# Attention's output kept as 512 rows with its sums apart, and a state tensor with its slots innermost

## The chip, the cores and the metric

The kernel runs on one core of a Trainium2 chip. The metric is the time of one execution on the device, in microseconds (us). The core has five engines with an instruction queue each: TensorE (PE; its weight loads are listed as PEld), VectorE (DVE), ScalarE (ACT), GpSimd (POOL) and SyncE (SP). SP computes nothing here; it issues nearly all DMA transfers, one after the other, and an instruction that waits holds up everything behind it in its queue. The same holds for the queues of the other engines.

## The reference

Two layers of a backbone over 1024 latent tokens with 256 context tokens in front, 1280 columns in all (T in the kernel). Only layer 0 is touched by the change. There attention and a state-space layer (S5) work side by side on parts of one projection, and their outputs are put together and projected:

```python
def _softmax_attend(q, k, v):
    s = einsum('bqhd,bkhd->bhqk', q, k) * MLA_SCALE
    return einsum('bhqk,bkhd->bqhd', softmax(s), v)          # 8 heads of 64 values

def _s5_states(u, lb_re, lb_im, bb_re, bb_im, h0):           # 32 groups, 64 complex states, two directions
    x_re, x_im = einsum(u, bb_re), einsum(u, bb_im)
    s_re, s_im = associative_scan(_s5_combine, (a, x))       # s[t] = lb * s[t-1] + x[t], complex

def s5_out(y, us):
    z = gelu(y + d_g * us)
    return z * sigmoid(z @ w_glu)

y_lat = concat([att_l, s5_out(ys_l, us_l)], -1) @ w_out      # and the same for the context tokens
```

Then come LayerNorm, a gated convolutional FFN, the second layer (HGRN2) and its FFN.

## The kernel before

All of it is one program; its instructions are put in order ahead of time, engine by engine, by a list scheduler that works with a model of durations. So the order on an engine is fixed when the kernel runs, and an edit can move instructions far from it. Large products are made of three fp32r matmuls on a high and a low part (`mm3`, L103 to L105; `split` at L111 and L114 makes the parts).

**Attention** (`attention`, L694). For each head `qk(h + 1)` (keys, queries, and the row maxima `mx`, L796) is interleaved with `attend(h)` (L811 on): for a block of up to 512 queries and every tile of 128 keys, three matmuls into `pS`, an Exp on ACT (L821), the split into `ph` and `pl` on ACT and on DVE or POOL in turn (L114), and three matmuls into `po` (L826 to L828). Row 64 of `po` is the sum of the exponentials. The block `ao`, 65 rows, goes to the DRAM tensor `attd[h]` (L834), which is 8 x 65 x 1280. `inverse` (L842) reads the sums of two heads from `attd` into `rsum`, 128 partitions of up to 20 numbers (L847), takes the reciprocal on DVE (L849) and writes it to the DRAM tensor `rsd` (L850). It is called after heads 1, 3 and 5, and for the last pair after each of the three blocks of head 7.

**S5** (`S5Half.run`, L883) is interleaved with the heads. It works on half of the groups at a time (`hh` = 0, 1), with 1280 columns in 160 chunks of 8. Per half:

- 8 steps of matmuls `pV` (L904) give the chunk inputs; ACT writes them to `H` (L907).
- A scan over the 160 chunks: two levels up (`both((0, 1), True)`), 38 sequential steps on POOL (L946, L948, L949), two levels down. In the levels direction 0 runs on DVE and direction 1 on POOL, each a product into `t` (L923) and two additions into `H` (L927). Tile `t` carries the tag of `RO` on DVE and of `Tm` on POOL, and is so named in the profile.
- 16 groups of matmuls `pY`: 4 that read `H` (L965) and one that reads `U` (L968). An fp32 matmul is two passes, so these are 8 and 2 PE instructions a group, 256 and 64 in all. Then a gelu on ACT and DVE (L969 to L974) and a write to the DRAM tensor `Zd` (L977). All groups share one PSUM bank.

`H` is 128 x 161 x 2 x 2 x 8: slot (chunk) outermost, then direction, real or imaginary part, and 8 group pairs innermost. One slot is 32 numbers, 128 bytes. So the scan's operands are runs of 16 or 8 neighbours, and a `pY` matmul reads 160 numbers that are 128 bytes apart.

**mix_out0** (L1191) follows. It loads `z` from `Zd` (L1200), and for each block of columns the attention values (`acc<-attd`, L1215, into a part of `acc` that is free then) and the reciprocals (`r<-rsd`, L1216). `zs` is the split of `z` on ACT (L1219) and DVE (L1220). The reciprocals are spread over partitions by a matmul with `sel` (`prs`, L1224) and multiplied on (L1226). `pglu` (L1232 on) is the gate product. `mix_out` (`pmix`) then makes the output projection. For the second and third block the loads at L1215 stand behind `k.last_inv` in the order (`behind`, L127).

Of the kernel before, what the change touches and what calls it, by code (L numbers as in the profile page):

```python
# [693 lines left out]
def attention(k, A):  # L694
# [115 lines left out]
    def attend(h):  # L810
        b = h % 2  # L811
        q, kk_, v = QT[b], KT[b], Vt[b]
        for s, e in BLK:
# [19 lines left out]
            nc.scalar.activation(o[0:65, :n], po[0:65, :n], AF.Copy)  # L833
            nc.sync.dma_start(out=k.attd[h, :, s:e], in_=o[0:65, :n])  # L834
            yield 1
            if h == 7:
                inverse(h, s, e)
        if h in (1, 3, 5):
            inverse(h, 0, T)
            yield 1  # L840

    def inverse(h, s, e):  # L842

        n = (e - s) // 64
        r = AO([128, 20], tag="rsum")
        a, o = k.attd, k.rsd
        nc.sync.dma_start(out=r[:, :n], in_=bass.AP(tensor=a.tensor, offset=a.offset + ((h - 1) * 65 + 64) * T + s,  # L847
                                                    ap=[[65 * T, 2], [n, 64], [1, n]]))
        nc.vector.reciprocal(r[:, :n], r[:, :n])  # L849
        k.last_inv = nc.sync.dma_start(out=bass.AP(tensor=o.tensor, offset=o.offset + (h - 1) * T + s,  # L850
                                                   ap=[[T, 2], [n, 64], [1, n]]), in_=r[:, :n])

# [18 lines left out]
class S5Half:  # L871
# [11 lines left out]
    def run(self):  # L883
        k, nc, P = self.k, self.k.nc, self.P
        E = nc.gpsimd
        for hh in range(2):
            U = P([128, 16, 160], tag="U")
            for j in range(8):
                nc.sync.dma_start(out=U[16 * j:16 * j + 16],
                                  in_=k.Sd[hh * 16:hh * 16 + 16, :, j].rearrange("g c x -> c g x"))  # L890
            H = P([128, 161, 2, 2, 8], tag="H")
            Mh = P([128, 3, 2, 2, 2, 8], tag="Mh")
# [4 lines left out]
            for p in range(8):  # L897
                RT = P([128, 2, 2, 128], tag="RO", bufs=2)
                nc.sync.dma_start(out=RT[:], in_=k.s5R[hh * 8 + p].rearrange("d i s x -> s d i x"))
                for d in range(2):  # L900
                    ps = bank(k, "pV", "D")
                    for i in range(2):
                        for q in range(2):
                            nc.tensor.matmul(ps[64 * q:64 * q + 64, i * 160:i * 160 + 160],  # L904
                                             lhsT=RT[:, d, i, 64 * q:64 * q + 64], rhs=U[:, 2 * p + q], start=True, stop=True)
                    o = 1 - d
                    nc.scalar.activation(H[:, o:o + 160, d, :, p].rearrange("p x i -> p i x"),  # L907
                                         ps[:, :320].rearrange("p (i x) -> p i x", i=2), AF.Copy)
# [4 lines left out]
            def bulk(i, up, d):  # L913
# [5 lines left out]
                for j in range(0, 80 // h, m):  # L919
                    n = min(m, 80 // h - j)  # L920
                    t = P([128, m, 2, 16], tag=tag, bufs=2 - d)[:, :n]
                    at = lambda s0, dims: raw(H, (s0 + 2 * h * j) * 32 + 16 * d, [[64 * h, n]] + dims)
                    e.tensor_tensor(t, Mh[:, i, d].rearrange("p a b q -> p a (b q)").unsqueeze(1)  # L923
                                    .to_broadcast([128, n, 2, 16]), at(src, [[0, 2], [1, 16]]), op=OP.mult)
                    o = at(dst, [[8, 2], [1, 8]])
                    for b in range(2):
# [8 lines left out]

            nc.vector.memset(H[:, 160, 1], 0.0)
            yield from both((0, 1), True)
            nc.vector.memset(H[:, 128, 0], 0.0)
            seq = [(128 + c, 132 + c, (132 + c) % 160) for c in range(4, 32, 4)] + [(c, c + 4, c + 4) for c in range(0, 124, 4)]
            seb = [(c + 4, c) for c in range(152, 0, -4)]  # L940
            assert len(seq) == len(seb)
            for (pf, cf, df), (pb, cb) in zip(seq, seb):
                sl = lambda f, b, dims: raw(H, f * 32, [[(b - f) * 32 + 16, 2]] + dims)
                t1 = P([128, 2, 2, 2, 8], tag="t1", bufs=2)
                t2 = P([128, 2, 16], tag="t2", bufs=2)
                E.tensor_tensor(t1[:].rearrange("p d a b q -> p d a (b q)"), Mh[:, 2].rearrange("p d a b q -> p d a (b q)"),  # L946
                                sl(pf, pb, [[0, 2], [1, 16]]), op=OP.mult)
                E.tensor_tensor(t2[:].rearrange("p d (a q) -> p d a q", a=2), t1[:, :, :, 0], t1[:, :, :, 1], op=OP.add)  # L948
                E.tensor_tensor(sl(df, cb, [[1, 16]]), t2[:], sl(cf, cb, [[1, 16]]), op=OP.add)  # L949
                yield 1  # L950
            yield from both((1, 0), False)
            for p in range(8):
# [8 lines left out]
                for q in range(2):  # L961
                    ps = bank(k, "pY", "D")
                    for d in range(2):
                        for i in range(2):
                            nc.tensor.matmul(ps[:, :160], lhsT=O[64 * q:64 * q + 64, d, i],  # L965
                                             rhs=H[64 * q:64 * q + 64, d:d + 160, d, i, p],
                                             start=d == 0 and i == 0, stop=False)
# [223 lines left out]
def mix_out0(k, A, u, acc):  # L1191
# [11 lines left out]
    for s, e in BLK:  # L1203
# [8 lines left out]
        for ct in range(4):  # L1212
            for i in range(n // w):
                with behind(k, k.last_inv if s else None):
                    nc.sync.dma_start(out=at[ct][:, i], in_=k.attd[2 * ct:2 * ct + 2, 0:64, s + i * w:s + i * w + w])  # L1215
        nc.sync.dma_start(out=rt[:, :n], in_=k.rsd[:, s:e])  # L1216
        zs = [G([128, 4, 512], R, tag=f"zs{i}", bufs=1) for i in range(2)]
# [332 lines left out]
def body(tc, A, out, stop=None, taps=None):  # L1550
# [11 lines left out]
    with ExitStack() as st:  # L1562
# [4 lines left out]
        k.Zd = tc.dram_tile([32, 16, 8, 160], F, name="Zd")  # L1567
        k.attd = tc.dram_tile([8, 65, T], F, name="attd")
        k.rsd = tc.dram_tile([8, T], F, name="rsd")
        wp = k.wip  # L1570
# [111 lines left out]
```

## Time and profile before

| what | value |
|---|---|
| time, median of 3 runs (lowest to highest) | 3838.55 us (3833.25 to 3847.12) |
| the profiled execution's own time | 3833.38 us |
| its span, first to last instruction | 3831.3 us |
| mean granted TensorE clock | 0.962 |
| busy: PE, DVE, ACT, POOL | 3622.7, 2061.9, 1090.9, 1135.5 us |

The times are of single executions. The span leaves out 2 us around the first and last instruction. The busy share of an engine is an average over stages with different limits; matmuls are pipelined, so a busy PE is not one at its best rate. The stage that the change touches, attention with S5 beside it and then mix_out0, lies between about 250 and 1030 us of the span.

### The profile page before, as it was taken

To read this page: it belongs to the slowest core of one execution; us is meant where nothing else is said; L and a number is where in the kernel's file an instruction comes from. 1 tells how busy PE (TensorE), PEld (TensorE's weight loads), DVE (VectorE), ACT (ScalarE), POOL (GpSimd) and SP (SyncE) were. 2 spreads that over 40 slices of the span, in tenths; PEclk is the share of its full clock that TensorE was granted. 3 is DMA by queue.
4 is the path that set the end of the run, shared out by engine and by line. 5 is a ranking of instruction groups with operands and counts; after the bars stand their busy time and mean duration, and the time that the engine had idled before them with its cause. 6 is when DMAs were issued, how large, how long until landed. Compare 5 with 4: busy or idle time off the path is not lost.

```text
span 3831.3 us, 47488 instructions
## 1 busy us (share of the span) xinstructions
PE 3622.7 (95%) x19081; PEld 2926.6 (76%) x19081; DVE 2061.9 (54%) x3297; ACT 1090.9 (28%) x1798; POOL 1135.5 (30%) x1089
## 2 busy tenths in 40 slices
PE   6987999997799999999999999999999999999997
PEld 4764566565588888888887888999987978888885
DVE  7836745773445444444446756464654654444445
ACT  2323435443323111121112422222222421212113
POOL 3617612851243111211113511111112622222222
PEclk9997989998899999999999999999998999999998
DMA  7462335312311111111110211111113111111111
GB/s 241 121 172 79 110 93 138 108 37 69 122 39 34 34 39 34 40 43 39 39 34 28 78 34 34 34 34 34 34 49 96 44 55 39 55 44 50 44 44 44
DMA packets 295583, 243.13 MB, mean 63 GB/s; under 512 B 42496, under 2 KB 256858, under 8 KB 294338
## 3 DMA queue, kind: packets, MB, share of 16 engines
q1 hardware_dynamic: 290434, 227.40, 20.0%
q10 hardware_dynamic: 4928, 12.69, 1.0%
q8 instruction: 150, 2.46, 0.3%
q14 instruction: 71, 0.58, 0.0%
HBM read 203.83 MB, written 38.32 MB: 63 GB/s over the span
## 4 chain that ended last, share of the span: by engine, by line
PE 83%; DVE 5%; DMA 3%; POOL 2%; issue 1%; ACT 1%; SPq 0%; ACTq 0%; POOLq 0%; DVEq 0%
PE pa L105 5%; PE pa L103 5%; PE pa L104 5%; PE po L103 5%; PE pg L103 5%; PE pg L105 5%; PE pg L104 5%; PE po L104 5%; PE po L105 5%; PE ph L104 3%; PE ph L105 3%; PE ph L103 3%; PE pA L1433 3%; PE pY L965 2%; PE pmix L103 1%; PE pmix L105 1%
## 5 line engine op out<-in xcount | busy, mean ns | idle before, releaser
L114 POOL TENSOR_TENSOR w<-ws,w 128x1024 fp32r<-128x1024 f32 (+1 forms) x205 | 500.9, 2449 | 1567.6 <-ACT w L111 1389.3
L1066 DVE SCALAR_TENSOR_TENSOR acc<-po,mod,acc 128x512 f32<-128x512 f32 (+1 forms) x456 | 309.3, 679 | 557.9 <-PE po L105 557.6
L103 PE MATMUL po<-hh,w 128*128 128x512 f32 (+1 forms) x912 | 342.1, 376 | 9.8 <-DVE acc L1066 8.1
L104 PE MATMUL po<-hl,w 128*128 128x512 f32 (+1 forms) x912 | 335.6, 368 | 6.0 <-DVE hl L114 6.0
L105 PE MATMUL po<-hh,w 128*128 128x512 f32 (+1 forms) x912 | 335.0, 368 | 0.0
L111 ACT ACTIVATE w<-ws 128x1024 fp32r<-128x1024 f32 (+1 forms) x207 | 216.9, 1049 | 409.9 <-PE pg L105 164.6
L103 PE MATMUL pa<-uh,w 128*128 128x512 f32 (+1 forms) x896 | 331.7, 370 | 0.9 <-ACT w L111 0.8
L104 PE MATMUL pa<-ul,w 128*128 128x512 f32 (+1 forms) x896 | 330.1, 369 | 0.1
L105 PE MATMUL pa<-uh,w 128*128 128x512 f32 (+1 forms) x896 | 326.4, 370 | 0.8 <-POOL w L114 0.8
L103 PE MATMUL pg<-uh,w 128*128 128x512 f32 (+1 forms) x872 | 324.1, 372 | 2.0 <-ACT w L111 2.0
L104 PE MATMUL pg<-ul,w 128*128 128x512 f32 (+1 forms) x872 | 322.6, 370 | 0.0
L105 PE MATMUL pg<-uh,w 128*128 128x512 f32 (+1 forms) x872 | 321.5, 372 | 0.6 <-POOL w L114 0.6
L103 PE MATMUL ph<-uh,w 128*128 128x512 f32 (+1 forms) x624 | 238.9, 383 | 1.1 <-ACT uh L1052 1.1
L104 PE MATMUL ph<-ul,w 128*128 128x512 f32 (+1 forms) x624 | 236.1, 378 | 1.3 <-DVE ul L1054 1.3
L105 PE MATMUL ph<-uh,w 128*128 128x512 f32 (+1 forms) x624 | 235.2, 377 | 0.0
L103 PEld LDWEIGHTS po<-hh,w 128*128 128x128 f32 x912 | 173.2, 190 | 45.3 <-DVE acc L1066 11.1
L104 PEld LDWEIGHTS po<-hl,w 128*128 128x128 f32 x912 | 173.9, 191 | 38.1 <-DVE hl L114 7.0
L105 PEld LDWEIGHTS po<-hh,w 128*128 128x128 f32 x912 | 173.7, 190 | 30.2
L103 PEld LDWEIGHTS pa<-uh,w 128*128 128x128 f32 x896 | 168.7, 188 | 32.7 <-ACT w L111 1.0
L105 PEld LDWEIGHTS pa<-uh,w 128*128 128x128 f32 x896 | 168.6, 188 | 32.2 <-POOL w L114 1.3
L104 PEld LDWEIGHTS pa<-ul,w 128*128 128x128 f32 x896 | 168.6, 188 | 32.2 <-DVE ul L1054 0.3
L103 PEld LDWEIGHTS pg<-uh,w 128*128 128x128 f32 x872 | 164.1, 188 | 35.6 <-ACT w L111 2.4
(401 smaller groups left out, 7914.6 us busy)
## 6 DMA issues: line engine op xcount, KB each, us to landing
ws<-in_ffn_w_in_dram SPq DMA_DIRECT2D x88, 512.0 KB
adaw<-in_ada_w_dram SPq DMA_DIRECT2D x80, 512.0 KB
ws<-in_ffn_w_out_dram SPq DMA_DIRECT2D x44, 512.0 KB
ws<-in_hg_w_in_dram SPq DMA_DIRECT2D x40, 512.0 KB
w<-in_ada_w_dram SPq DMA_DIRECT2D x8, 1024.0 KB
ws<-in_ev_w_out_dram SPq DMA_DIRECT2D x10, 512.0 KB
ws<-in_hg_w_out_dram SPq DMA_DIRECT2D x10, 512.0 KB
ws<-in_ev_w_in_dram SPq DMA_DIRECT2D x9, 512.0 KB
```

What stands on the lines that cost most here:

```text
L103: nc.tensor.matmul(ps, lhsT=w[0], rhs=x[0], start=start, stop=False)
L104: nc.tensor.matmul(ps, lhsT=w[0], rhs=x[1], start=False, stop=False)
L105: return nc.tensor.matmul(ps, lhsT=w[1], rhs=x[0], start=False, stop=stop)
L111: nc.scalar.activation(hi, src, AF.Copy)
L114: (nc.gpsimd if elo == "p" else nc.vector).tensor_tensor(lo, src, hi.bitcast(F), op=OP.subtract)
L965: nc.tensor.matmul(ps[:, :160], lhsT=O[64 * q:64 * q + 64, d, i], rhs=H[64 * q:64 * q + 64, d:d + 160, d, i, p], start=d == 0 and i == 0, ...
L1066: k.nc.vector.scalar_tensor_tensor(a, ps[:, :e - s], modcol(k, layer, seg, 1 if s >= SEQ else 0, ct), a, op0=OP.mult, op1=OP.add)
L1433: nc.tensor.matmul(ps[:, i * 128:i * 128 + 128], lhsT=km[:, c:c + 128], rhs=raw(Q, c, [[2 * hs, 64 // hs], [SEQ + hs, 2], [1, hs]]), start ...
```

## The change

Two independent edits.

1. `attd` becomes 512 x 1280 (head and value as rows), and the sums go to a tensor of their own, `atts`, 8 x 1280: each block is written by two DMAs, of 64 rows and of 1 row. `inverse` is gone. `mix_out0` loads 128 rows of `attd` at a time, loads the sums as 8 rows, and takes the reciprocal there, on the tile of 8 partitions x up to 512. The loads of the later blocks stand behind `k.last_sum`, the last write of sums.
2. `H` becomes 128 x 2 x 2 x 8 x 161: direction, part, pair, and the slot innermost. Neighbours in the slot are adjacent; neighbours in the pair are 161 numbers (644 bytes) apart. Every operand of `H` is rewritten for that; counts and sizes of instructions stay.

```diff
-            nc.sync.dma_start(out=k.attd[h, :, s:e], in_=o[0:65, :n])
+            nc.sync.dma_start(out=k.attd[64 * h:64 * h + 64, s:e], in_=o[0:64, :n])
+            k.last_sum = nc.sync.dma_start(out=k.atts[h:h + 1, s:e], in_=o[64:65, :n])
             yield 1
-            if h == 7:
-                inverse(h, s, e)
-        if h in (1, 3, 5):
-            inverse(h, 0, T)
-            yield 1
...
-            H = P([128, 161, 2, 2, 8], tag="H")
+            H = P([128, 2, 2, 8, 161], tag="H")
...
-                    nc.scalar.activation(H[:, o:o + 160, d, :, p].rearrange("p x i -> p i x"),
+                    nc.scalar.activation(H[:, d, :, p, o:o + 160],
...
-                    at = lambda s0, dims: raw(H, (s0 + 2 * h * j) * 32 + 16 * d, [[64 * h, n]] + dims)
+                    at = lambda s0, dims: raw(H, s0 + 2 * h * j + 16 * 161 * d, [[2 * h, n]] + dims)
-                                    .to_broadcast([128, n, 2, 16]), at(src, [[0, 2], [1, 16]]), op=OP.mult)
-                    o = at(dst, [[8, 2], [1, 8]])
+                                    .to_broadcast([128, n, 2, 16]), at(src, [[0, 2], [161, 16]]), op=OP.mult)
+                    o = at(dst, [[8 * 161, 2], [161, 8]])
...
-                E.tensor_tensor(sl(df, cb, [[1, 16]]), t2[:], sl(cf, cb, [[1, 16]]), op=OP.add)
+                E.tensor_tensor(sl(df, cb, [[161, 16]]), t2[:], sl(cf, cb, [[161, 16]]), op=OP.add)
...
-                                             rhs=H[64 * q:64 * q + 64, d:d + 160, d, i, p],
+                                             rhs=H[64 * q:64 * q + 64, d, i, p, d:d + 160],
...
-                with behind(k, k.last_inv if s else None):
-                    nc.sync.dma_start(out=at[ct][:, i], in_=k.attd[2 * ct:2 * ct + 2, 0:64, s + i * w:s + i * w + w])
-        nc.sync.dma_start(out=rt[:, :n], in_=k.rsd[:, s:e])
+                with behind(k, k.last_sum if s else None):
+                    nc.sync.dma_start(out=at[ct][:, i], in_=k.attd[128 * ct:128 * ct + 128, s + i * w:s + i * w + w])
+        nc.sync.dma_start(out=rt[:, :n], in_=k.atts[:, s:e])
+        nc.vector.reciprocal(rt[:, :n], rt[:, :n])
...
-        k.attd = tc.dram_tile([8, 65, T], F, name="attd")
-        k.rsd = tc.dram_tile([8, T], F, name="rsd")
+        k.attd = tc.dram_tile([512, T], F, name="attd")
+        k.atts = tc.dram_tile([8, T], F, name="atts")
```

The scheduler gives the attention stage a new order. Outside it, nearly nothing moves. Three places matter.

SP's queue at the end of attention, before: the writes of the last two blocks of head 7, the loads of attention values, and the reads and writes of `inverse` stand ahead of the load of `z`.

```order
L834 DMA attd<-ao 65x512
L1215 DMA acc<-attd 128x1x512
L847 DMA rsum<-attd 128x1x8
L834 DMA attd<-ao 65x256
L1215 DMA acc<-attd 128x1x512
L850 DMA rsd<-rsum 2x64x8
L1215 DMA acc<-attd 128x1x512 x2
L847 DMA rsum<-attd 128x1x4
L850 DMA rsd<-rsum 2x64x4
L1215 DMA acc<-attd 128x1x256 x2
L1200 DMA z<-Zd 128x1280 x4
```

The same place now (L962 is the write to `Zd`, L1200 the load of attention values, L1185 the load of `z`):

```order
L834 DMA attd<-ao 64x256
L943 DMA RO<-s5O 128x4x128
L835 DMA atts<-ao 1x256
L1200 DMA acc<-attd 128x512
L1200 DMA acc<-attd 128x256 x2
L962 DMA Zd<-z 8x16x160 x2
L1200 DMA acc<-attd 128x256 x6
L962 DMA Zd<-z 8x16x160 x4
L1185 DMA z<-Zd 128x1280 x4
```

The chain through `rsum` and `rsd` is gone; the last three pairs of writes to `Zd`, which stood ahead of the last block of attention, now stand behind it.

PE at the end of attention, before: the last group of `pY` (L965, L968), the last tiles of head 7, and the first `pglu`.

```order
L965 MATMUL pY<-H,RO 128x160 x4
L968 MATMUL pY<-U,Tm 128x160
...
L826 MATMUL po<-ph,V_2164 128x256
L827 MATMUL po<-ph,V_2165 64x256
L828 MATMUL po<-pl,V_2164 128x256
L103 MATMUL pglu<-zs_8214,w 128x512 x2
```

And now (L950 and L953 are the two kinds of `pY`); the pair of `pY` rows comes six times behind the last tile of attention:

```order
L826 MATMUL po<-ph,V_2164 128x256
L827 MATMUL po<-ph,V_2165 64x256
L828 MATMUL po<-pl,V_2164 128x256
L950 MATMUL pY<-H,RO 128x160 x4
L953 MATMUL pY<-U,Tm 128x160
...
L103 MATMUL pglu<-zs_8215,w 128x512 x2
```

Six of the 16 groups of the second half have moved behind attention. Counted in tiles of `attend` (176 in all), the first `pY` of the two halves stands behind tile 36 and 154 now, where it stood behind 32 and 142.

DVE at the start of mix_out0, before: two reciprocals of `inverse`, then the splits of `z`.

```order
L849 RECIPROCAL rsum<-rsum 128x8
L849 RECIPROCAL rsum<-rsum 128x4
L1220 TENSOR_TENSOR zs_8215<-z,zs_8214 128x512 x4
L1226 TENSOR_TENSOR rt<-acc,prs 128x512 x2
L1237 TENSOR_TENSOR sg<-sg,z 128x512
```

And now (L1206 is the split, L1202 the reciprocal, L1212 the product with `prs`, L1223 the gate):

```order
L1206 TENSOR_TENSOR zs_8216<-z,zs_8215 128x512 x3
L1202 RECIPROCAL r_8208<-r_8208 8x512
L1206 TENSOR_TENSOR zs_8216<-z,zs_8215 128x512
L1212 TENSOR_TENSOR rt<-acc,prs 128x512 x2
L1223 TENSOR_TENSOR sg<-sg,z 128x512
L1212 TENSOR_TENSOR rt<-acc,prs 128x512
L1223 TENSOR_TENSOR sg<-sg,z 128x512
L114 TENSOR_TENSOR ul<-sg,uh 128x512
L1212 TENSOR_TENSOR rt<-acc,prs 128x512
L1202 RECIPROCAL r_8322<-r_8322 8x512
```

The reciprocals stand between the splits and the products of the blocks, each behind a load of 8 rows.

## Rows read from the trace of the kernel before

**Rows 1.** Busy us (count) of each engine, clock, DMA: stretches of PE's matmuls.
```profile
452.00:578.00 126.00, 126.00 (x541) 77.94 (x540) 59.99 (x104) 49.20 (x106) 21.62 (x24) 0.91 0.33 95
716.00:785.00 69.00, 68.36 (x386) 43.48 (x386) 45.09 (x80) 37.68 (x71) 58.66 (x132) 1.00 0.34 104
835.00:927.00 92.00, 92.00 (x353) 64.60 (x352) 40.07 (x65) 43.13 (x96) 17.23 (x13) 0.89 0.24 68
933.00:972.00 39.00, 0.00 (x0) 0.00 (x0) 0.38 (x2) 1.04 (x2) 0.00 (x0) 0.51 0.33 107
```

**Rows 2.** The same for the first of the scan's four level stretches, and their sum.
```profile
306.00:340.00 34.00, 18.31 (x61) 10.16 (x61) 31.96 (x47) 5.81 (x10) 26.64 (x27) 0.59 0.10 27
...
sum 171.00, PE 135.09 PEld 84.11 DVE 156.04 ACT 66.10 POOL 136.77; mean PE 33.77 PEld 21.03 DVE 39.01 ACT 16.52 POOL 34.19
```

**Rows 3.** Chain that ended last, end of attention: start us, us, what.
```profile
932.22 2.29 DMA attd<-ao
934.53 6.63 DMA rsum<-attd
...
941.42 6.05 DMA rsd<-rsum
947.49 10.42 DMA rsum<-attd
...
959.88 11.45 DMA z<-Zd
```

**Rows 4.** ACT in order of time, the last of the four splits of z.
```profile
976.76 1.12 ACT L1219 ACTIVATE zs<-z 128x512 fp32r<-128x512 f32 x1 [0.53 <-DMA z<-Zd]
```

**Rows 5.** PE in order of time: start us, us; one group of pY.
```profile
463.77 2.42 PE L965 MATMUL pY<-H,RO 64*128 64x160 f32 x8
466.12 0.54 PE L968 MATMUL pY<-U,Tm 128*128 128x160 f32 x2
```

**Rows 6.** The same: fp32 passes over 128 neighbouring numbers, in layer 1.
```profile
2264.68 1.95 PE L1455 MATMUL pO<-AT,V 128*128 128x128 f32 x16
2266.46 0.49 PE L1472 MATMUL pT<-ident,K 128*128 128x128 f32 x3
```

**Rows 7.** Groups by form, the scan: xcount | busy us, mean ns | idle before.
```profile
L927 DVE TENSOR_TENSOR H<-H,RO 128x256 f32<-128x256 f32 x56 | 46.4, 840 | 0.3
L923 DVE TENSOR_TENSOR RO<-Mh,H 128x512 f32<-128x512 f32 x28 | 25.9, 929 | 4.0 <-POOL H L949 3.6 <-ACT H L907 0.4
...
L927 POOL TENSOR_TENSOR H<-H,Tm 128x320 f32<-128x320 f32 x48 | 50.9, 1060 | 2.4
L923 POOL TENSOR_TENSOR Tm<-Mh,H 128x640 f32<-128x640 f32 x24 | 42.7, 1778 | 3.0 <-ACT H L907 1.7
L946 POOL TENSOR_TENSOR t<-Mh,H 128x64 f32<-128x64 f32 x76 | 28.5, 376 | 5.2
L949 POOL TENSOR_TENSOR H<-t,H 128x32 f32<-128x32 f32 x76 | 24.6, 323 | 5.0
```

**Rows 8.** Groups by form, DVE at L1443: steps of 8 and of 16 bytes.
```profile
L1443 DVE TENSOR_TENSOR F<-F 128x1280 f32<-128x1280 f32 x8 | 11.9, 1489 | 0.2
L1443 DVE TENSOR_TENSOR F<-F 128x640 f32<-128x640 f32 x8 | 10.8, 1352 | 0.2
```

**Rows 9.** Groups by form, ACT from PSUM: steps of 128 bytes, and none.
```profile
L907 ACT ACTIVATE H<-pV 128x320 f32<-128x320 f32 x32 | 23.7, 740 | 27.4 <-PE pV L904 26.8 <-ACT vo L728 0.4
L1474 ACT ACTIVATE kt<-pT 128x384 f32<-128x384 f32 x48 | 23.3, 488 | 58.7 <-PE pT L1472 58.6
```

**Rows 10.** Busy us (count), clock, DMA share, GB/s; mix_out0's first block.
```profile
985.00:990.00 5.00, 5.00 (x21) 3.69 (x20) 5.00 (x6) 3.27 (x6) 2.68 (x2) 1.00 0.13 44
```

**Rows 11.** SP in order of time: six loads of attention values.
```profile
969.91 21.30 SPq L1215 DMA_DIRECT2D acc<-attd  x6
```

**Rows 12.** PE in order of time: the second block's reciprocals.
```profile
1000.98 2.90 PE L1224 MATMUL prs<-r,sel 8*128 8x512 f32 x3 [8.21 <-DMA r<-rsd]
```

**Rows 13.** Groups by form, DVE's reciprocals.
```profile
L849 DVE RECIPROCAL rsum<-rsum 128x8 f32<-128x8 f32 x2 | 0.4, 203 | 10.4 <-DMA rsum<-attd 10.4
L434 DVE RECIPROCAL sm<-sm 128x32 f32<-128x32 f32 x1 | 0.3, 347 | 0.0
```

More of the change, by code (lines that the diff above doesn't have):

```diff
@@ L833, in attend @@
             nc.scalar.activation(o[0:65, :n], po[0:65, :n], AF.Copy)
-            nc.sync.dma_start(out=k.attd[h, :, s:e], in_=o[0:65, :n])
+            nc.sync.dma_start(out=k.attd[64 * h:64 * h + 64, s:e], in_=o[0:64, :n])
+            k.last_sum = nc.sync.dma_start(out=k.atts[h:h + 1, s:e], in_=o[64:65, :n])
             yield 1
-            if h == 7:
-                inverse(h, s, e)
-        if h in (1, 3, 5):
-            inverse(h, 0, T)
-            yield 1
[L842 to L851, printed above, removed]
     AD = Pool(k, "ada1", "right")
@@ L934, in both @@
                     yield 1
-            nc.vector.memset(H[:, 160, 1], 0.0)
+            nc.vector.memset(H[:, 1, :, :, 160], 0.0)
             yield from both((0, 1), True)
-            nc.vector.memset(H[:, 128, 0], 0.0)
+            nc.vector.memset(H[:, 0, :, :, 128], 0.0)
             seq = [(128 + c, 132 + c, (132 + c) % 160) for c in range(4, 32, 4)] + [(c, c + 4, c + 4) for c in range(0, 124, 4)]
@@ L942, in run @@
             for (pf, cf, df), (pb, cb) in zip(seq, seb):
-                sl = lambda f, b, dims: raw(H, f * 32, [[(b - f) * 32 + 16, 2]] + dims)
+                sl = lambda f, b, dims: raw(H, f, [[b - f + 16 * 161, 2]] + dims)
                 t1 = P([128, 2, 2, 2, 8], tag="t1", bufs=2)
@@ L946, in run @@
                 E.tensor_tensor(t1[:].rearrange("p d a b q -> p d a (b q)"), Mh[:, 2].rearrange("p d a b q -> p d a (b q)"),
-                                sl(pf, pb, [[0, 2], [1, 16]]), op=OP.mult)
+                                sl(pf, pb, [[0, 2], [161, 16]]), op=OP.mult)
                 E.tensor_tensor(t2[:].rearrange("p d (a q) -> p d a q", a=2), t1[:, :, :, 0], t1[:, :, :, 1], op=OP.add)
-                E.tensor_tensor(sl(df, cb, [[1, 16]]), t2[:], sl(cf, cb, [[1, 16]]), op=OP.add)
+                E.tensor_tensor(sl(df, cb, [[161, 16]]), t2[:], sl(cf, cb, [[161, 16]]), op=OP.add)
                 yield 1
```

## The prediction

> **What bounds the kernel now.** I read the busy times by stretch first. In 452 to 578 us and 835 to 927 us, where the `pY` groups stand between attention's tiles, PE is busy all the time, DVE less than half, POOL under a fifth [rows 1]: PE sets the pace. In the sequential scan (716 to 785 us) it is busy 68.36 of 69 us, with POOL at 58.66. In the four stretches of the scan's levels it is not: of 171 us DVE is busy 156.04, POOL 136.77, PE 135.09, and in the first of them PE only 18.31 of 34 [rows 2]; there attention's own DVE work queues behind the scan's. From 933 to 972 us PE does nothing [rows 1]. The chain of waits tells why [rows 3]: the last block of sums is read back (6.63 us), written (6.05 us), the next read lands 10.42 us after its issue, and only then does SP reach the load of `z`, which takes 11.45 us more. The last split of `z` starts at 976.76 us [rows 4].
>
> **Part 1: `pY` reads neighbours.** A pass of L965 takes (466.12 - 463.77) / 8 = 0.294 us for 160 numbers 128 bytes apart [rows 5]. An fp32 pass over 128 neighbours takes (2266.46 - 2264.68) / 16 = 0.111 us [rows 6], so 0.139 us for 160. The difference is 0.155 us, over 256 passes 39.7 us. Both ends: nothing, if the width of 64 rows and not the step makes these passes slow; 39.7 us otherwise. I take the latter, since 0.294 is twice what the count asks for. Of the 32 groups 26 still lie ahead of attention's end: 26 x 8 x 0.155 = 32.2 us. The six that moved behind it leave that stretch wholly: 6 x (2.35 + 0.54) = 17.3 us. Together 49.5 us of PE's queue. PE bounds most of the stretch but not the levels, where its share is 135/171 = 0.79; I count 0.8 of it: **-40 us** (between -50 and -25).
>
> **Part 2: the scan walks in steps of 644 bytes.** Every operand of `H` on DVE and POOL was a run of 8 or 16. At L1443 all three operands have one step: at 8 bytes 1489 / 1280 = 1.16 ns a number, at 16 bytes 1352 / 640 = 2.11 [rows 8]. So +0.95 ns for each number. On DVE these are L923 (28 of 512 and 4 of 256) and L927 (56 of 256 and 8 of 128) [rows 7], 30,720 numbers: +29 us. For POOL no row shows a long step. Its bounds: nothing, since at 1060 / 320 = 3.3 ns a number [rows 7] a slower fetch may hide behind its own pace; a doubling, as PE and DVE show it, +147 us on the 50.9 + 42.7 + 28.5 + 24.6 us. I take ACT's price for such a step, since ACT is the nearest engine with a row: 740 ns for 320 numbers at 128 bytes, against 488 x 320 / 384 = 407 without [rows 9], 1.0 ns a number, rounded down to 0.9 because POOL is slow already: 38,016 numbers, +34 us, of which 28 in the levels and 7 in the sequential part. The latter lies beside PE's work at 58.66 of 69 us: nothing.
>
> In the levels it is not hidden. DVE's 29 and POOL's 28 us come on stretches where both are nearly full. Side by side they cost 29 us, one after the other 57; since a DVE addition of 256 numbers takes 840 ns [rows 7] where L1443's rate gives 300, they stand in each other's way already, so I take 40. PE is not idle all that time; its own work there waits in order for DVE's maxima and splits. I count half: **+20 us** (0 to 57). What is hidden: the two halves' first `pY` stand 4 and 12 tiles later in the order, which gives the scan room.
>
> [...]
>
> ACT's write to `H` gets the other way: 32 x (740 - 407) ns = 10.7 us less on ACT, in front of the scan. ACT is at 49.20 of 126 us at most [rows 1]; I cost it at nothing.
>
> **Part 3: the end of attention.** Count from 933 us, where PE stops. Before, the last split of `z` starts 43.8 us later [rows 4]. Now the six groups come first: 10 passes x 0.139 plus some 0.7 us until ACT has emptied their one bank (estimate from ACT's 488 ns for 384 [rows 9]), 2.1 us each, 12.6 us. The gelu adds about 2 us (four such small operations), the issue of the last writes 1.2 and their landing 2.3, as for `attd<-ao` [rows 3]: 18 us. The first three loads of `z` need not wait for the landing. From the first issue to the last split it is 976.76 - 959.88 = 16.9 us before, with loads of attention values beside it. So 16 + 16 = 32 us, **-12 us** (-20 to -3). If ACT or the `Zd` writes hold the groups up (two buffers of `z`), it is 38.
>
> **Part 4: mix_out0.** Three reciprocals move into DVE's queue. From 8 to 32 numbers one goes from 203 to 347 ns [rows 13], 6.0 ns a number: 3.2 us for 512, twice, and 1.7 for 256, 8.1 us. Each stands behind a load just issued, and behind it on DVE wait the products with `prs` and the gate, for which PE waits: all on the path if nothing covers it, some 12 us with the loads. Against it, PE's wait of 8.21 us for the second block's reciprocals [rows 12] had six loads of attention values in front, 21.30 / 6 = 3.55 us each [rows 11], with a DMA share of 0.13 at 44 GB/s [rows 10]: two of sixteen engines. Now 128 rows are the outermost dimension, where 2 heads were. I take these as even: **0** (-8 to +12). The first reciprocal delays the last split's DVE half by 3 us; that is in it. The 24 extra writes of a row of sums, and the 12 small transfers, 6 reciprocals and their waits that go, are off the path except as counted.
>
> [...]
>
> **Sum.** -40 + 20 - 12 + 0 = -32 us, off the profiled execution's 3833.38: 3801. That execution is 5 us under the median of the three, so 3806 us as a median. About 0.3%, 11.5 us, is what a measurement of this kernel can tell from no change.
>
> **Rivals.**
> - *The step costs POOL little* and the levels stay as they are: -50 + 0 - 15 = -65, with part 4 at +5: 3778 us. For it: POOL's own slow pace. Against it: all three other engines pay. 0.13.
> [...]
> - *Slower: POOL doubles, and PE waits at the first `pY`.* The order is fixed, so PE stands there, with attention's tiles behind it, until the scan is done. Chain +147 + 29 = 176 us; the room is 16 tiles at (835 - 452) / 122 = 3.1 us, 50 us. PE waits 126 us, against -50 - 12 of gains: +64, 3903 us. It decides from about +112 us of chain, POOL at 1.6 times its time. For it: PE's and DVE's doubling. Against: POOL's slow pace, and part of the chain lies beside other POOL work. 0.08.
> - *The loads stay on two engines.* Ten of them stand ahead of the load of `z`, 10 x 3.55 us, half of it behind the six groups: +17, 3823 us. Against: rows 10. 0.04.
>
> The forecast has 0.60. Its own range is 3785 to 3825; with the cases beside it, 3775 to 3841. Chances: faster 0.60 - 0.03 (its upper tail) + 0.13 + 0.04 + 0.02 = 0.76; same 0.03 + 0.10 = 0.13; slower 0.08 + 0.03 = 0.11.
>
> **What would show it.** Right: passes of `pY` at 0.14 us between neighbours; DVE's additions at L912 up from 840 ns by 0.2 to 0.3 us; no transfer of `rsum`; PE idle after attention for 15 to 22 us, not 39, behind six groups 2 us apart; loads of attention values done in under 2 us; two reciprocals of 3.2 us. Wrong: POOL's level operations at twice their time, PE idle in front of a first `pY`, or the same gap behind attention with another name.

## The result and the profile after

The changed kernel takes 3790.93 us (median of 4, 3789.89 to 3792.65) against 3841.26 us (3833.25 to 3847.12): a ratio of 0.9871, 95% interval 0.9851 to 0.9891, or 50 us less. Measured again beside the experiments it was 0.9890 (0.9872 to 0.9908), 42 us less. The forecast was 3806 us, 32 less, in a range of 3775 to 3841. Between the two profiled executions the span went from 3831.3 to 3788.1 us, 43.2 less, and that is what the traces can explain:

| mark in the trace | before | after | forecast of the step | traces | again |
|---|---|---|---|---|---|
| PE leaves attention's last tile | 933 | 904.8 | -40 + 20 = -20 | -28 | -25 |
| from there to the last split of `z` | 43.8 | 29.4 | -12 | -14 | -12 |
| the rest of the span | | | 0 | -1 | -5 |

The last column is a second profiled execution of the changed kernel (e10_after_again): a step of one trace holds to some 3 or 4 us. In the rest of the span two things offset each other. From the first `pglu` to the last of the 576 `pmix` matmuls mix_out0 takes 174.9 us (again 173.8) instead of 182.0. What follows it, where the change touches nothing, takes 2683.0 us (again 2680.0) instead of 2676.8, and 2675 to 2685 in the traces of the other experiments.

Busy time by stretch after, in the windows of [rows 1] (start and end, length, PE, PEld, DVE, ACT, POOL busy us with counts, granted clock, DMA share, GB/s):

```profile
452.00:578.00 126.00, 122.50 (x655) 80.62 (x655) 82.53 (x129) 60.48 (x130) 45.89 (x43) 0.97 0.43 124
716.00:785.00 69.00, 67.14 (x355) 43.39 (x354) 46.14 (x79) 37.04 (x69) 58.02 (x107) 0.95 0.31 90
835.00:927.00 92.00, 79.44 (x378) 60.14 (x376) 48.95 (x69) 46.41 (x105) 33.52 (x24) 0.89 0.38 108
933.00:972.00 39.00, 38.50 (x119) 24.25 (x119) 32.71 (x29) 19.66 (x28) 16.15 (x9) 0.85 0.36 124
```

In the first, 655 instructions of PE stand where 541 stood. The third holds the rest of attention, six groups of `pY` and most of the gap; from 933 to 972 us PE now does mix_out0, where it did nothing. The first of the four level stretches, and their sum, against [rows 2]:

```profile
306.00:340.00 34.00, 12.59 (x39) 6.89 (x35) 33.81 (x37) 1.55 (x3) 30.55 (x24) 0.61 0.06 13
...
sum 171.00, PE 120.30 PEld 74.80 DVE 157.29 ACT 54.78 POOL 143.21; mean PE 30.07 PEld 18.70 DVE 39.32 ACT 13.69 POOL 35.80
```

DVE and POOL were nearly full and still are; PE gets 15 us less done in the same 171. These are the windows of [rows 2]; the scan is longer now, and a part of its last levels lies behind them. The scan lasts 172 and 185 us in the two halves, instead of 146 and 162. Its groups by form, against [rows 7] (count | busy us, mean ns | idle before):

```profile
L912 POOL TENSOR_TENSOR H<-H,Tm 128x320 f32<-128x320 f32 x48 | 67.0, 1397 | 2.2
L908 POOL TENSOR_TENSOR Tm<-Mh,H 128x640 f32<-128x640 f32 x24 | 55.5, 2313 | 0.9
L912 DVE TENSOR_TENSOR H<-H,RO 128x256 f32<-128x256 f32 x56 | 54.4, 982 | 3.4 <-POOL H L934 3.1
L908 DVE TENSOR_TENSOR RO<-Mh,H 128x512 f32<-128x512 f32 x28 | 45.7, 1632 | 4.7 <-POOL H L934 4.2 <-ACT H L892 0.5
L931 POOL TENSOR_TENSOR t<-Mh,H 128x64 f32<-128x64 f32 x76 | 33.9, 446 | 5.0
L892 ACT ACTIVATE H<-pV 128x320 f32<-128x320 f32 x32 | 14.0, 436 | 27.1 <-PE pV L889 26.6 <-ACT vo L728 0.4
```

The rows of POOL here are 16.1, 12.8 and 5.4 us longer, 34 in all, the two of DVE 8.0 and 19.8, 28 in all; ACT's copy is 9.7 us shorter. PE in order of time at the end of attention, against [rows 5] and the empty stretch of [rows 1]:

```profile
904.47 0.28 PE L828 MATMUL po<-pl,V 128*128 128x256 f32 x1
904.68 1.35 PE L950 MATMUL pY<-H,RO 64*128 64x160 f32 x8
905.96 0.54 PE L953 MATMUL pY<-U,Tm 128*128 128x160 f32 x2
...
914.31 2.50 PE L950 MATMUL pY<-H,RO 64*128 64x160 f32 x8 [0.59 <-ACT zt L955]
916.74 0.90 PE L953 MATMUL pY<-U,Tm 128*128 128x160 f32 x2
...
920.65 0.90 PE L953 MATMUL pY<-U,Tm 128*128 128x160 f32 x2
930.25 1.22 PE L103 MATMUL pglu<-zs,w 128*128 128x512 f32 x2 [8.70 <-ACT zs L1205]
```

A pass takes (905.96 - 904.68) / 8 = 0.160 us, where it took 0.294. Six groups follow the last tile, and then PE waits 8.70 us. Before, it waited 39.53:

```profile
972.46 1.22 PE L103 MATMUL pglu<-zs,w 128*128 128x512 f32 x2 [39.53 <-ACT zs L1219]
```

SP in order of time, against [rows 11], and ACT's fourth split of `z`, against [rows 4]:

```profile
912.36 2.82 SPq L1200 DMA_DIRECT2D acc<-attd  x6
915.84 9.08 SPq L962 DMA_DIRECT2D Zd<-z  x4
925.02 2.18 SPq L1185 DMA_DIRECT2D z<-Zd  x4
```
```profile
934.13 1.14 ACT L1205 ACTIVATE zs<-z 128x512 fp32r<-128x512 f32 x1 [0.65 <-DMA z<-Zd]
```

Six loads of attention's values, 128 KB each, leave SP in 2.82 us, where six of that size held it for 21.30; the load of `z` goes out at 925.02 us and not at 959.88. The reciprocals, against [rows 13]:

```profile
L1202 DVE RECIPROCAL r<-r 8x512 f32<-8x512 f32 x2 | 6.7, 3338 | 0.0
L1202 DVE RECIPROCAL r<-r 8x256 f32<-8x256 f32 x1 | 1.7, 1733 | 0.0
```

### The profile page after: what moved, and what is told of

Read it like the earlier page. It is cut to its first block, busy times and chain, and to the rows that moved or that the text cites. A ratio compares the mean times of both kernels' runs of the same rounds, so it can differ in the third digit from the quotient of the medians.

```text
span 3788.1 us, 47489 instructions
## 1 busy us (share of the span) xinstructions
PE 3588.2 (95%) x19081; PEld 2910.3 (77%) x19081; DVE 2101.3 (55%) x3294; ACT 1082.7 (29%) x1798; POOL 1178.5 (31%) x1089
## 4 chain that ended last, share of the span: by engine, by line
PE 82%; DVE 7%; POOL 2%; DMA 2%; issue 1%; ACT 1%; SPq 0%; ACTq 0%; POOLq 0%; DVEq 0%
PE pa L105 5%; PE po L103 5%; PE pa L103 5%; PE pa L104 5%; PE po L104 5%; PE po L105 5%; PE pg L103 5%; PE pg L105 5%; PE pg L104 5%; PE ph L104 3%; PE ph L105 3%; PE ph L103 3%; PE pA L1419 3%; PE pmix L103 2%; PE pmix L104 2%; PE pmix L105 2%
## 5 line engine op out<-in xcount | busy, mean ns | idle before, releaser
L105 PEld LDWEIGHTS po<-hh,w 128*128 128x128 f32 x912 | 173.8, 191 | 30.2
L105 PEld LDWEIGHTS pa<-uh,w 128*128 128x128 f32 x896 | 168.6, 188 | 32.2 <-POOL w L114 1.3
L104 PEld LDWEIGHTS pa<-ul,w 128*128 128x128 f32 x896 | 168.6, 188 | 32.2 <-DVE ul L1039 0.3
```

Of the source, the lines that this page charges most:

```text
L104: nc.tensor.matmul(ps, lhsT=w[0], rhs=x[1], start=False, stop=False)
L105: return nc.tensor.matmul(ps, lhsT=w[1], rhs=x[0], start=False, stop=stop)
```

## The experiments

Each kernel was timed beside the kernel before on the same chip. "Less" is (1 - ratio) times the median of before there (3830 to 3833 us). e1 to e8 ran on one chip, e9 to e11 on a second, e12 on a third, so a difference between two rows can go across chips. The theory at the start was the prediction's, with its four parts.

| kernel | scan's steps | `pY` reads | loads' outermost | chain of inverses | us less (95%) |
|---|---|---|---|---|---|
| e1_h_only | far | near | 2 heads | yes | 15 (10 to 20) |
| e2_sums_only | near | far | 128 rows | no | 34 (28 to 40) |
| e12_loads_only | near | far | 128 rows | yes | 28 (23 to 34) |
| e6_two_heads_out | far | near | 2 heads | no | 8 (3 to 12) |
| e9_chain_kept | far | near | 128 rows | yes | 44 (38 to 51) |
| changed kernel (e10_after_again) | far | near | 128 rows | no | 42 (35 to 49) |
| e3_near_scan | near | near | 128 rows | no | 81 (76 to 86) |
| e5_act_far | near | near | 128 rows | no | 78 (71 to 86) |
| e4_slots_inner | 8, 16 bytes | near | 128 rows | no | 74 (69 to 79) |
| e7_no_inverse | 8, 16 bytes | near | 128 rows | no | 79 (72 to 86) |
| e8_z_first | 8, 16 bytes | near | 128 rows | no | 84 (76 to 91) |
| e11_best_again (e8 again) | 8, 16 bytes | near | 128 rows | no | 79 (72 to 85) |

**H alone.** The new `S5Half.run` in the kernel before:

```diff
-            H = P([128, 161, 2, 2, 8], tag="H")
+            H = P([128, 2, 2, 8, 161], tag="H")
 ... (and its readers; attend, inverse and mix_out0 as before)
```

> Only the tile H with its slots innermost; the heads' sums go the old way (65 rows a head, read back, inverted, written). Theory (both parts of the change pay, as forecast): the passes of pY at 0.16 us as in the changed kernel, the scan 24 us a half longer, attention's last tile 20 to 28 us earlier (after 905 to 913 us instead of 933), and behind it the old chain of transfers with PE idle for about 39 us less the few pY groups that the order puts there: 3841 - 28 = 3813 us. Rival A (all of the gain is the sums; H is even, its longer scan eats what pY gives): 3841 us, attention ends at 930 to 935 us. Rival B (H alone carries it): 3795 us.

15 us less. Attention ends at 908.4 us, 24.5 earlier, as the theory said, but 17 of these are lost behind it: the first `pglu` starts 7 us earlier than before. The other 8 come in mix_out0, which takes 173.7 us and not 182.0; there PE waits 2.5 us for the second block's reciprocals and not 8.21 [rows 12]. SP and PE in order of time:

```profile
937.62 14.61 SPq L1215 DMA_DIRECT2D acc<-attd  x6
952.33 3.50 SPq L977 DMA_DIRECT2D Zd<-z  x2
955.93 7.07 SPq L1200 DMA_DIRECT2D z<-Zd  x4
```
```profile
927.81 2.50 PE L965 MATMUL pY<-H,RO 64*128 64x160 f32 x8 [8.21 <-ACT zt L970]
930.24 0.90 PE L968 MATMUL pY<-U,Tm 128*128 128x160 f32 x2
965.24 1.22 PE L103 MATMUL pglu<-zs,w 128*128 128x512 f32 x2 [34.10 <-ACT zs L1219]
```

The last writes of `Zd` and the load of `z` stand in SP's queue behind loads of attention's values that SP lets go at one every 2.4 us (six in 14.61). The theory took the groups off the old wait of 39 us; but PE waits 8.21 us among them and 34.10 behind them. That pointed at the loads.

**The sums alone.** The rest of the change, with the old `S5Half.run`:

```diff
-            nc.sync.dma_start(out=k.attd[h, :, s:e], in_=o[0:65, :n])
+            nc.sync.dma_start(out=k.attd[64 * h:64 * h + 64, s:e], in_=o[0:64, :n])
+            k.last_sum = nc.sync.dma_start(out=k.atts[h:h + 1, s:e], in_=o[64:65, :n])
 ... (inverse taken out; mix_out0 as in the change)
```

> Only the sums in a tensor of 8 rows and the heads as 512 rows, with H as before. Theory: attention ends at 932 us as before; the load of z goes out at once, PE is idle 6 to 10 us instead of 39.5, mix_out0 takes 2 us less: -34 us, 3807 us. Since the two parts share the gap behind attention (six pY groups stand in it in the changed kernel), the sum of the two gains, -28 and -34, is more than the -50 of both together. Rival A: 3791 us, as the changed kernel. Rival B (the gap is another wait, for the writes of Zd or the loads of attention's values, and stays near 30 us): 3830 us.

34 us less, as the theory had it. PE waits 12.13 us behind attention, a little more than the 6 to 10 expected:

```profile
945.33 1.22 PE L103 MATMUL pglu<-zs,w 128*128 128x512 f32 x2 [12.13 <-ACT zs L1205]
```

The expectation that the two parts share a gain was not borne out: 15 + 34 = 49, against 42 to 50 for both.

**The scan's steps taken away.**

```diff
-at = lambda s0, dims: raw(H, s0 + 2 * h * j + 16 * 161 * d, [[2 * h, n]] + dims)
+at = lambda s0, dims: raw(H, (s0 + 2 * h * j) * 32 + 16 * d, [[64 * h, n]] + dims)
-at(src, [[0, 2], [161, 16]])
+at(src, [[0, 2], [1, 16]])
 ... (likewise in the additions, the sequential steps and the two memsets; two small memsets more)
```

> The changed kernel, but the scan walks the memory of H in the old steps (runs of 8 and 16 neighbours) while the copies into H and the reads of pY keep the new layout, so that the scan works on mixed-up numbers: the price of the scan's 644-byte steps taken away, nothing else. Theory (the scan's longer steps cost time, forecast +20 us, and push six groups behind attention): the scan as long as before (146 and 162 us), attention ends 27 us before the old 932.9 with all groups inside it, gap 8 us: 3841 - 27 - 32 - 2 = 3780 us, 11 us under the changed kernel. Rival (the steps are hidden beside PE's work and cost nothing): 3791 us as the changed kernel. Rival (they cost their full 50 us of scan): 3745 us.

81 us less, where the theory of this run had 61 and its second rival 96; so the long steps cost the changed kernel 32 to 39 us, by its two measurements: more than the 20 of the forecast, less than the 50 by which the scan is longer. The scan is back at 148.5 and 164.3 us, and no group stands behind attention.

**Slots innermost in the loops too.**

```diff
-t = P([128, m, 2, 16], tag=tag, bufs=2 - d)[:, :n]
+t = P([128, 2, 16, m], tag=tag, bufs=2 - d)[:, :, :, :n]
-at = lambda s0, dims: raw(H, s0 + 2 * h * j + 16 * 161 * d, [[2 * h, n]] + dims)
+at = lambda s0, dims: raw(H, s0 + 2 * h * j + 16 * 161 * d, dims + [[2 * h, n]])
 ... (the product's other operand and the additions to match)
```

> The changed kernel with the loops of the scan's level operations turned round: slots run innermost (steps of 8 bytes in level 0, 16 in level 1) and the 16 numbers of a slot outside, products kept in the same order; same sums. Theory (the price is one of the step in bytes, DVE paid 1.16 ns a number at 8 bytes and 2.11 at 16): DVE's products of 512 numbers fall from 1632 ns to about 700 in level 0 and stay near 1100 to 1600 in level 1, the scan shortens by 10 to 20 us a half: 3783 us. Rival (any step that is not a neighbour costs the same, 644 bytes or 8): durations as in the changed kernel, 3791 us. Rival (short inner loops at the old place gave POOL its speed, and POOL gets slower): 3800 us.

74 us less, 24 to 31 better than the changed kernel, where the theory had 8. The groups by form:

```profile
L912 POOL TENSOR_TENSOR H<-H,Tm 128x320 f32<-128x320 f32 x48 | 57.0, 1187 | 2.4
L912 DVE TENSOR_TENSOR H<-H,RO 128x256 f32<-128x256 f32 x56 | 44.8, 815 | 5.7 <-POOL H L934 5.5
L908 POOL TENSOR_TENSOR Tm<-Mh,H 128x640 f32<-128x640 f32 x24 | 38.6, 1608 | 1.1
L908 DVE TENSOR_TENSOR RO<-Mh,H 128x512 f32<-128x512 f32 x28 | 31.7, 1135 | 0.1
```

Every group is well under its mean in the changed kernel, and two of the four are under [rows 7]. So the price goes with the step of the innermost loop. That loop also has more turns now than 8 or 16, and no run parts the two; but short loops were not what gave POOL its speed, since its product is faster than before the change. The scan takes 150 and 161.5 us, as before the change to within 4. This version beats both kernels.

**ACT's copy with its old step**, in e3:

```diff
-nc.scalar.activation(H[:, d, :, p, o:o + 160],
+nc.scalar.activation(raw(H, o * 32 + 16 * d + p, [[8, 2], [32, 160]]),
```

> As e3_near_scan (near scan, near reads of pY, numbers mixed up), with ACT's 32 copies into H also put back to steps of 128 bytes (740 ns in place of 434 each, +9.8 us of ACT). e3 was 80 us under the kernel before. Theory (the prediction's nothing for this term was wrong: pV and the copy take turns on one bank, so it lies on the path): 70 us under the kernel before, the two stretches of pV some 5 us longer each. Rival (hidden, as the prediction had it): 80 us under.

78 us less (71 to 86) against 81 (76 to 86) for e3, and attention's last tile starts no later (884.9 us against 886.4): no price of the 9.8 us of ACT shows, as the prediction had it. The theory of this run, 70, lies just outside. The kernel gives something more: it differs from e2_sums_only in the reads of `pY` alone (and two small memsets a half), so these are worth 78 - 34 = 44 us, give or take 10. The stretches of `pY`, first in e2 (far), then in e5 (near):

```profile
455.00:578.00 123.00, 123.00 (x544) 76.53 (x542) 61.97 (x104) 49.47 (x107) 22.50 (x26) 0.94 0.34 99
829.00:933.00 104.00, 103.15 (x398) 71.71 (x396) 46.52 (x73) 50.65 (x112) 21.76 (x17) 0.90 0.23 66
```
```profile
452.00:550.00 98.00, 98.00 (x520) 64.79 (x519) 56.85 (x98) 47.01 (x105) 22.12 (x26) 1.00 0.41 121
797.00:885.00 88.00, 86.12 (x439) 65.25 (x436) 54.86 (x80) 57.25 (x125) 23.14 (x18) 1.00 0.28 81
```

They shrink by 25 and 16 us. PE's own passes give about 256 x 0.134 = 34 of that; the rest goes with the granted clock, 0.94 and 0.90 with far reads, 1.00 with near ones.

**The form of the loads.** The changed kernel, with 65 rows a head again and the sums still apart:

```diff
-in_=k.attd[128 * ct:128 * ct + 128, s + i * w:s + i * w + w])
+in_=k.attd[2 * ct:2 * ct + 2, 0:64, s + i * w:s + i * w + w])
-k.attd = tc.dram_tile([512, T], F, name="attd")
+k.attd = tc.dram_tile([8, 65, T], F, name="attd")
```

> The changed kernel (49 us under the kernel before), but the heads' values kept in a tensor of 65 rows a head again, so that a load's outermost dimension is 2 heads and not 128 rows; the sums stay in 8 rows of their own, inverted on load. Theory (the loads' form matters: as in e1_h_only SP issues one each 2.85 us, ten of them and the last writes of Zd stand ahead of the load of z): +17 to +25 us, so 24 to 32 us under the kernel before, with the gap behind attention the longer by this. Rival (only the chain of inverses mattered, the loads are hidden): no change, 49 us under.

8 us less, not 42 to 50: this one edit costs 34 to 42 us, more than the theory's 25, and by itself takes away nearly all that the change gains. SP, a stretch of it, and ACT and PE:

```profile
924.89 21.06 SPq L1200 DMA_DIRECT2D acc<-attd  x7
946.05 3.88 SPq L962 DMA_DIRECT2D Zd<-z  x2
...
954.38 6.08 SPq L1185 DMA_DIRECT2D z<-Zd  x4
```
```profile
925.00:945.00 20.00, 7.31 (x22) 5.44 (x22) 1.97 (x4) 2.43 (x8) 0.00 (x0) 0.50 0.15 52
```
```profile
921.78 0.30 ACT L954 ACTIVATE z<-pY 128x160 f32<-128x160 f32 x1 [8.51 <-DMA Zd<-z]
922.33 2.50 PE L950 MATMUL pY<-H,RO 64*128 64x160 f32 x8 [7.91 <-ACT zt L955]
...
962.80 1.22 PE L103 MATMUL pglu<-zs,w 128*128 128x512 f32 x2 [24.49 <-ACT zs L1205]
```

The transfers run at a share of 0.15 and 52 GB/s, as in [rows 10]; SP, which let the first three loads go in some 0.55 us each, gives out one in 3.0 us here. The writes of `Zd` stand behind them, so the two buffers of `z` stay taken, ACT can't empty the bank of `pY` (it waits 8.51 us for `Zd`, and PE for it 7.91 us in the middle of the six groups), and the load of `z` goes out 29 us later than in the changed kernel. In that kernel the share is 0.83 at 248 GB/s:

```profile
909.00:916.00 7.00, 5.33 (x26) 4.50 (x27) 1.97 (x4) 2.38 (x8) 0.00 (x0) 0.86 0.83 248
```

**The chain put back, with the new loads**, first in the changed kernel, then with the old `H`:

```diff
+            if h == 7:
+                inverse(h, s, e)
 ... (inverse as before, reading k.atts and writing k.rsd)
-        nc.sync.dma_start(out=rt[:, :n], in_=k.atts[:, s:e])
-        nc.vector.reciprocal(rt[:, :n], rt[:, :n])
+        nc.sync.dma_start(out=rt[:, :n], in_=k.rsd[:, s:e])
```

> The changed kernel (49 us under the kernel before) with the old chain put back: the sums read from their 8 rows, inverted on 128 partitions, written to rsd and read again; the heads' values stay 512 rows, loaded with 128 rows outermost. With e6_two_heads_out (8 us under) it splits the sums' part in two: the form of the loads and the chain. Theory (the form of the loads is nearly all of it; with the queue clear each hop of the chain takes some 2 us, and the six groups of pY cover it; 8 us of reciprocals go the other way): within 8 us of the changed kernel, 41 to 52 us under the kernel before. Rival (the chain by itself costs what the prediction's part 3 was about): 30 us under or less.

> The kernel before with the form of the loads alone: heads as 512 rows and sums in 8 rows of their own, but H in its old layout and the old chain (sums read back, inverted, written, read again). e2_sums_only, without the chain, was 34 us under the kernel before. Theory (the form of the loads is the gain, and once it is right the chain's hops take 2 to 3.5 us as in e9_chain_kept; here no pY group covers them, and the load of z stands behind two of them): 27 to 34 us under, the gap behind attention 12 to 18 us in place of 39.5. Rival (the chain is what held the load of z in the old layout, where nothing covers it): 15 us under or less, gap of 25 us or more.

44 and 28 us less: with the chain the time is that of the changed kernel (42 beside it), and with the old `H` it is 5 us over e2's, within both intervals. The chain of waits in e12, where nothing covers it (start us, us, what), against [rows 3]:

```profile
929.47 2.56 DMA rsum<-atts
932.36 2.22 DMA rsd<-rsum
934.60 2.04 DMA rsum<-atts
...
938.50 6.82 DMA z<-Zd
```

The same transfers took 6.63, 6.05 and 10.42 us in the kernel before. There four loads of attention's values, 256 KB each, were issued among them (932.96 to 946.54 us), and from 941 to 958 us the DMA engines moved 46 GB/s at a share of 0.13. In e12 nothing but the form of the loads and the tensors of values and sums differs, and the write to `rsd`, the same in both, took 2.22 us and not 6.05: these loads made the transfers long. The chain is not quite free in e12. PE waits 18.72 us behind attention and not e2's 12.13, a little over the 12 to 18 expected; some 4 us come back in mix_out0, which has no reciprocals then:

```profile
946.46 0.80 PE L103 MATMUL pglu<-zs,w 128*128 128x512 f32 x1 [18.72 <-ACT zs L1220]
```

For the new `H` the runs make a square. With loads of 2 heads the kernel is 15 us under the one before with the chain (e1) and 8 without it (e6); with loads of 128 rows it is 44 with the chain (e9) and 42 to 50 without it. So the form of the loads is worth 29 to 42 us with the chain or without, and taking the chain out gains nothing that can be told with either form. For the old `H` the kernel without the chain, but with the old loads, was not run.

**The reciprocals left out**, in e4:

```diff
-nc.vector.reciprocal(rt[:, :n], rt[:, :n])
+pass
```

> e4_slots_inner (73 us under the kernel before) without the three reciprocals on DVE: the products are made with the sums themselves, the inversion is left out. It gives the price of the reciprocals in mix_out0. Theory (3.3 + 3.3 + 1.7 us stand in DVE's queue with PE waiting behind them; 8 us at most): 3 to 8 us less, 76 to 81 us under. Rival (hidden beside PE's work, as PE is busy 49.5 of 50 us there): 73 us under.

79 against 74 us less: the intervals overlap, and by the times alone the price lies between nothing and some 10 us. The traces are closer. From the first `pglu` to the last of the 576 `pmix` matmuls, eight executions with the three reciprocals and the new loads take 173.1 to 175.1 us (the changed kernel twice, e2 to e5, e8, e11), and the three without them 169.8, 170.3 and 170.6 (e12, e9, e7): 3 to 5 us.

**The load of `z` first**, in e4:

```diff
-with behind(k, k.last_sum if s else None):
+with behind(k, k.last_sum if s else zl):
```

> e4_slots_inner (73 us under the kernel before) with the loads of attention's values for the first block ordered behind the loads of z, which go out some 2 to 3 us earlier and share the DMA engines with fewer others. Theory (the load of z ends the gap behind attention): 2 to 5 us less, 75 to 78 us under. Rival (the values come too late for the first products, DVE and PE wait there): 70 us under.

84 us less, where the theory had 75 to 78, and 79 when run again (below). PE waits 8.5 us behind attention instead of e4's 11.1; the intervals of the two runs overlap, so no more than these 2.6 us is shown.

**Both again on one chip.**

> The changed kernel itself, beside the others on this chip: 49 us under the kernel before by the first measurement, 45 to 53 expected.

> e8_z_first again, beside the changed kernel on one chip: 81 us under the kernel before by its first measurement, so 30 to 34 us under the changed kernel. If the two are within 25 us, the price of the scan's long steps that e3 and e4 showed was taken across chips wrongly.

3789.11 and 3752.20 us. The changed kernel is 42 us under the kernel before, a little less than the 45 to 53 expected; the version with the slots innermost in the loops and `z` first is 37 us under the changed kernel and 79 under the kernel before.

## Why the prediction came out right, and where its steps were not

- **Part 1, -40 (-50 to -25).** The mechanism was right: it was the step and not the 64 rows that made the passes slow, and the reads of `pY` are worth 44 us (e2 against e5). That the size fits is in part luck. Of the -40 only 0.8 x 32.2 = 26 us are faster reads; the other 14 are the six groups that leave the stretch, and part 3 takes them on again with 12.6. A pass takes 0.160 us and not 0.139, so PE saves 34 us and not 39.7. Against that the sum did not have the granted clock of the `pY` stretches, which was 0.94 and 0.90 in e2 and 1.00 in e5.
- **Part 2, +20 (0 to 57).** The mechanism was right, but the term was mis-sized: the steps cost 32 to 39 us (e3). The scan became 50 us longer, where the sum had 40, and about 35 of these come out in the time, so the line that fails is "I count half"; why more than half comes out no run shows. The busy times came out nearly as forecast, DVE +28 us (29) and POOL +34 (34), POOL's by luck. The shortest operation of each group, which comes nearest to the step's own price, went from 673 to 1069 ns for DVE's product and from 354 to 603 for its addition, 0.8 and 1.0 ns a number (forecast 0.95). POOL's went from 1524 to 1852 and from 847 to 1012 ns, 0.5 ns a number and not 0.9: by these some 18 of the 34 us, an estimate. The rest came while both engines were busy: in the changed kernel 22 of POOL's 24 products had DVE at work beside them for over 80% of their time and took 2350 ns on average, and the one that had it for under 20% took 1901.
- **POOL's rise.** POOL's products went from 1778 to 2313 ns on average, 30%, and its additions from 1060 to 1397, 32%, with DVE at work beside most of them; the shortest product went up by 22%.
- **ACT's copy at nothing.** Right as far as e5 can tell.
- **Part 3, -12 (-20 to -3).** The size was right, 14 and 12 in the two traces, the reason wrong, and this is the step that failed: "The chain of waits tells why [rows 3]". The chain of inverses was a victim. Put back, with the loads in their new form, it costs nothing that can be measured (e9), or 5 us uncovered, within the intervals (e12). Inside the part, the six groups took 16.8 us and not 12.6, mostly since the last two ran at a granted clock of 0.50 (2.50 us for eight passes against 1.35). From the load's issue to the last split it took 9.1 us and not 16; no loads of attention's values lay beside it any more, which fits.
- **Part 4, 0 (-8 to +12).** Inside its range, but not even: mix_out0 is 7 us shorter (8 in the second trace). The wait of 8.21 us is gone, and the reciprocals cost 3 to 5 us (e7); they took 3.34, 3.34 and 1.73 us, close to what was worked out from [rows 13]. In the span it does not show, since what follows took 6 us longer in this trace. And the sum weighed the loads' form only against PE's wait inside mix_out0. Its place is ahead of that: a dozen loads in SP's queue among the last writes of `Zd` and ahead of the load of `z`.
- **The rival "the loads stay on two engines", +17.** It did not happen, and its price was half of what e6 shows, 34 to 42 us. "Half of it behind the six groups" was the error: the groups themselves wait for SP through the buffers of `z`. In the traces the loads over 2 outermost rows go with a share of 0.13 (44 GB/s [rows 10], two packets of the DMA engines under way at a time for 84% of that stretch, three for the rest) and of 0.15 (52 GB/s, e6), the loads over 128 rows with 0.83 (248 GB/s in the changed kernel, 12 to 17 packets at a time for 67% of 909 to 916 us).
- **The other rivals.** That the step costs POOL little did not come true, though the time lies as near to that rival's 3778 as to the forecast: POOL paid 34 us. The one in which POOL doubles would have ended at 3903 us; POOL's rise was 30%, that rival's threshold 60%. The forecast and the three rivals of 0.13, 0.08 and 0.04 make 0.85; the other 0.15 of the chances stand for a case with some 60 us more in POOL's levels, and no run shows that price: their two groups took 16.1 and 12.8 us more in the changed kernel. PE never waited for the scan in front of a `pY`; its waits there, 2.9 us in all, were for ACT. The room in the order was enough.
- **The signs.** Passes at 0.160 us (0.14 was said), DVE's additions up by 0.14 us (0.2 to 0.3), the groups 2.4 and at the end 3.9 us apart (2), PE idle behind them for 8.7 us (15 to 22). All go the way that was said, and none of them could tell the chain from the loads.

By edit, then, the split was the other way round. The forecast gave H 20 of its 32 us and the sums 12. By the runs H is worth 8 to 16 (the changed kernel less e2, e9 less e12; 15 in e1) and the sums 34 (e2), of which the form of the loads is 28 (e12). In the trace it looks as forecast, because the six groups that H pushed behind attention took 17 us out of the one stretch and into the other. So the time came out in part by luck: the price of the steps was 12 to 19 us too small, and the gain of the sums 22.

What stays open: how the 32 to 39 us of the long steps divide between DVE and POOL, and what the chain costs by itself beside the old `H` and the old loads.

## What to carry to other kernels

When small transfers in a chain take 6 to 10 us each, look first at what else stands in their queue and moves at the same time, and try the chain with that traffic made fast, before the chain is taken out. Several loads in a row whose outermost dimension is 2 held the queue here (seven for 21.06 us, e6), and with it every write behind them and the buffers these free. When a layout is turned for one reader, try turning the loops of the others as well, so that their innermost step stays short: here that was worth 24 to 31 us, more than the new layout of H had given by itself, in five lines. And when a forecast has several terms, take them apart by runs even where the total fits: here two errors of some 15 and 22 us hid each other.

## What the hardware showed that was not expected

- In a row of loads of 128 KB over 2 outermost rows SP took 3.0 us for each (7 in 21.06 us), over 128 rows 0.47 (6 in 2.82). The shape alone does not hold SP: the first three over 2 rows, 256 KB each, went out in 0.53 to 0.57 us (e6), and a row of six over 128 rows, right behind the load of `z`, took 8.24 us and not 2.82 (e12).
- An fp32 matmul pass on 64 rows over 160 neighbours takes 0.160 us; over numbers 128 bytes apart 0.294, and the granted clock of such a stretch was 0.90 to 0.94 (e2) instead of 1.00 (e5). At a granted clock of 0.50 the two cost the same: 0.304 us for neighbours (914.31 in the changed kernel) and 0.306 at 128 bytes, here in the kernel before:

```profile
532.56 2.52 PE L965 MATMUL pY<-H,RO 64*128 64x160 f32 x8
535.01 0.90 PE L968 MATMUL pY<-U,Tm 128*128 128x160 f32 x2
```

- A step of 644 bytes costs DVE's product of 512 numbers 703 ns on average (396 by the shortest) and POOL's of 640 535 ns (328 by the shortest). With a step of 8 or 16 bytes and long inner loops POOL's product, 1608 ns, is faster than with runs of 16 neighbours, 1778.
